# A hybrid decoder trunk: running sums carried in the accumulators, and the spatial gate's loads one block ahead

## The chip, the cores and the metric

The kernel runs on one core of a Trainium2 chip. The metric is device time in microseconds (us), and the figure for a kernel is the median of its timed executions. One further execution was taken under the hardware profiler. Its trace says when each instruction of each engine ran, and every row shown below comes from it.

The engines: TensorE (PE) multiplies matrices into PSUM, a memory of accumulators. VectorE (DVE) and ScalarE (ACT) work elementwise on SBUF and PSUM. SyncE (SP) issues the DMA transfers. Each engine works through its own queue in order.

## The reference

Two decoder layers run over 256 tokens of width 2048, in float32. The change lies in layer 0: in its input projection with the spatial gating that follows, and in its feed-forward network (FFN).

```
def swiglu(h, w_gate, w_up, w_down):
    a = silu(h @ w_gate) * (h @ w_up)
    return a @ w_down

def chunked_spatial_gating(u, v, ln_g, ln_b, w_s, b_s):
    v = layer_norm(v, ln_g, ln_b).reshape(bsz, n_chunks, 128, 16, 128)
    w = where(causal, w_s, 0.0)
    mixed = einsum('hts,bcshe->bcthe', w, v) + b_s.T[:, :, None]
    return u * mixed

def ab_mixer(hm, ...):
    u, v, z, xbc, dt_raw = split(hm @ w_in)
    y_a = chunked_spatial_gating(gelu(u), gelu(v), ...)
    y_b = ssd_mixer(z, xbc, dt_raw, ...)     # conv and silu of xbc, scan, silu(z)
    return concatenate([y_a, y_b]) @ w_out

# per layer
hm = rms_norm(x) * (1 + sc_m) + sh_m         # sc, sh, g: silu(c) @ ada_w + ada_b
x = x + (1 + g_m) * mixer(hm)
hf = rms_norm(x) * (1 + sc_f) + sh_f
x = x + (1 + g_f) * swiglu(hf)
```

## The kernel before

Every large product runs on TensorE in three passes. Weights and activations are split into a high and a low part: ScalarE rounds a slab of weights to its high part (`hi`, line 330), VectorE subtracts to get the low part (`lo`, line 335), and TensorE sums high by high, high by low and low by high in PSUM. A slab has up to two k tiles of 128 rows and 512 columns. `wslab` (line 320) loads it from SP into one of four `raw` buffers; `hi` and `lo` have three buffers each. A block is 512 output columns for all 256 tokens and fills one accumulator of 128 x 1024 in the pool `psA`, which has two. `dense_ws` keeps weights stationary and `dense_as` activations; their products are lines 396 and 162.

The modulation of a layer (`ada_w`) is itself streamed and summed on VectorE in the background (`ada_unit`, line 207). The first layer's input projection cannot wait for all of it. So `grouped` (line 548) cuts the 16 k tiles into groups of 4, 5 and 7 (`GROUPS`) and runs all 14 blocks of `ORDER` (six x, four v, four z) over the first group, then over the second, then over the third. The activations of a group are made at its start (`begin`, `adaln`, line 529). The running sum of a block rests in SBUF: after the first group ScalarE copies the accumulator out (line 584), after each later group VectorE adds the accumulator to it (line 586). Only behind the last group's add does `finish(i)` run. For a layer-0 input block that is `finish0`: the convolution and Silu of an x block (lines 861 to 869), Gelu of a v block with sums for the layer norm (line 987), Silu of a z block (line 990). The first six gate and six up blocks of the FFN of layer 0 go through the same function in two groups of 8 k tiles, with `finishf` (Silu, and product of the pair, lines 1308 and 1311). That is 14 copies and 28 adds in the first stage, 12 and 12 in the second.

The spatial gate is worked in behind chosen blocks. After block 9 of the third group (`LN_AT`) `layer_norm` reduces the sums, squares the four v tiles on ScalarE and takes a square root (lines 933 to 943). After blocks 9, 11, 12 and 13 (`GM_AT`) `layer_norm_apply(b)` loads gain and bias and applies them on VectorE (lines 952, 953), and `spatial(b)` loads four heads of 128 x 128 spatial weights (line 957), transposes them on TensorE (line 960), masks them on VectorE (line 962) and multiplies. These three loads are issued where they are used, into the pool `t2` with six buffers.

A planner places the instructions of each engine at build time, by their order in the program and by priorities (`tc.high_priority`), and that order is fixed in each queue. `tc.issue_after` puts an instruction behind another one on its engine.

Of the kernel before, what the change touches and what calls it, by code (L numbers as in the profile page):

```python
# [46 lines left out]
DEFER = 6  # L47
ORDER = ("x4", "v0", "x5", "v1", "x0", "v2", "x1", "v3", "x2", "z0", "x3", "z1", "z2", "z3")
LN_AT = 9
GM_AT = (9, 11, 12, 13)  # L50
SSD_AT = (12, 14, 18, 20)


# [1 line left out]
def trunk(ctx: ExitStack, tc: tile.TileContext, x, c, norm_mix_g, norm_ffn_g, ada_w, ada_b,  # L55
# [134 lines left out]
    def ada_unit(layer, base, stride, width, dst, nr=2):  # L190

        side = 2 if nr == 1 else 1
        wide = side * width
        nk = max(1, 1024 // wide)
        row = ada_w.shape[2]
        acc = adp.tile([P, 1024], F32, tag="acc", name="acc", bufs=2)[:, 0:wide]

        def use(raw, g0):  # L200
            for i in range(nk):
                g = g0 + i
                r = raw[:, i * wide:(i + 1) * wide]
                if g == 0:
                    V.tensor_scalar(acc, r, ct[nr][:, g:g + 1], None, op0=OP.mult)
                else:
                    V.scalar_tensor_tensor(acc, r, ct[nr][:, g:g + 1], acc, op0=OP.mult, op1=OP.add)  # L207

        def end():
            n = width // P  # L210
            if nr == 1:
                first_mod.append(acc)
                return
            total = tmp.tile([P, 32], F32, tag="tot", name="tot", bufs=2)[:, 0:nr * n]
            for j0 in range(0, n, 4):
                m = min(4, n - j0)
                ps = pm()
                for j in range(m):
                    transpose(ps[:, j * P:(j + 1) * P], acc[:, (j0 + j) * P:(j0 + j + 1) * P])
                V.tensor_reduce(total[:, nr * j0:nr * (j0 + m)].rearrange("p (j b) -> p j b", b=nr),  # L220
                                ps[:, 0:m * P].rearrange("p (j r b) -> p j b r", j=m, b=nr), axis=AX.X, op=OP.add)
            for b, (sec, k0) in enumerate(dst):
                r = total[:, b:nr * n:nr]
                V.scalar_tensor_tensor(mod[layer][sec][:, k0:k0 + n], r, 0.0 if sec in (0, 3) else 1.0,
                                       adab[layer][:, sec * KT + k0:sec * KT + k0 + n], op0=OP.add, op1=OP.add)
                have.update((layer, sec, k) for k in range(k0, k0 + n))
            if dst[0][0] in (2, 5):
                gate_to_rows(layer, dst[0][0])

        for g0 in range(0, KT * nr, nk):  # L230
            raw = (bt() if nr == 1 and g0 not in FIRST_A else
                   adp.tile([P, 1024], F32, tag="araw", name="araw", bufs=A_BUFS))
            for i in range(nk):
                r = raw[:, i * wide:(i + 1) * wide]
                if nr == 1:
                    r = r.rearrange("p (b n) -> p b n", b=2)
                off = ada_w.offset + (layer * D + (g0 + i) * (P // nr)) * row + base
                t = nc.sync.dma_start(r, bass.AP(tensor=ada_w.tensor, offset=off,
                                                 ap=[[row, P // nr], [stride, max(nr, 2)], [1, width]]))
                if nr == 1:  # L240
                    wlast[0] = t
            landed.append((slab[0], lambda raw=raw, g0=g0: use(raw, g0)))
            yield raw
        landed.append((slab[0], end))
# [130 lines left out]
        for j in js:  # L375
            preps.append(lambda j=j: turn(j, src[j // 2], make))

    def dense_ws(w, c0, ks, ahead=W_AHEAD):

        acc = psA.tile([P, 1024], F32, tag="acc", name="accps").rearrange("p (n t) -> p n t", n=4)  # L380
        done = 0
        for run in slabs(ks):
            run_prep()
            hi, lo = wslab(w, run[0][0], len(run), c0, 512, ahead)
            ops = []
            for i, (_, (bh, bl)) in enumerate(run):
                done += 1
                ops += [(hi[:, i, :], bh, done == 1, False), (hi[:, i, :], bl, False, False),
                        (lo[:, i, :], bh, False, done == len(ks))]
            if done <= 2:  # L390
                order = [(n, o) for i in (0, 2, 1) for n in range(4) for o in ops[i:i + 1]] \
                    + [(n, o) for n in range(4) for o in ops[3:]]
            else:
                order = [(n, o) for i in range(0, len(ops), 3) for n in range(4) for o in ops[i:i + 3]]
            for n, (a, b, first, final) in order:
                dense_mm[0] = T.matmul(acc[:, n, :], a[:, n * P:(n + 1) * P], b, start=first and n % 2 == 0,  # L396
                                       stop=final, skip_group_check=True)
            if done >= min(DEFER, len(ks)):
                run_later()
            pump()  # L400
        return acc
# [12 lines left out]
            with tc.issue_after(dense_mm[0].ins):  # L414
                dense_mm[0] = held.pop(0)()

    def dense_as(w, c0, ks, ahead=W_AHEAD, head=None, tail=False, hold=False):

        if tail:
            accs = [pm(), pm()]
        else:
            full = psA.tile([P, 1024], F32, tag="acc", name="accps").rearrange("p (n t) -> p n t", n=2)
            accs = [full[:, 0, :], full[:, 1, :]]
        runs = list(slabs(ks))
        parts = [runs[:2]] if head else []
# [3 lines left out]
        for pi, part in enumerate(parts):  # L431
# [15 lines left out]
            for n, j, (r, i, x) in order:  # L447
# [6 lines left out]

                def product(n=n, j=j, i=i, x=x, bh=bh, bl=bl, hi=hi, lo=lo, last=pi == len(parts) - 1):
                    return mm(accs[n], (bl if x == 1 else bh)[:, n * P:(n + 1) * P], (lo if x == 2 else hi)[:, i, :],
                              first=pi == 0 and j == 0, last=last and j == len(ops) - 1)

                if hold and len(part) > 1 and n == 1 and j >= len(ops) - 2:
                    held.append(product)  # L460
# [84 lines left out]
    xs = []  # L545
    fdst = []

    def grouped(blocks, groups, layer, sh, make, finish, rates, lags, heads=None, early=0):


        hs = []
# [1 line left out]
        def begin(gi):  # L553
# [5 lines left out]
                new_pace(QUIET if sh else 0)  # L559
            hs.extend(make(k0, kg))  # L560

        for gi, (k0, kg) in enumerate(groups):
            if not (early and gi):
                begin(gi)
# [3 lines left out]
            for i, (dense, w, c0, dst) in enumerate(blocks):  # L568
                if early and not last and i == len(blocks) - early:
                    begin(gi + 1)  # L570
                args = {"head": heads} if heads and gi == 0 and i == 0 else {}
                if not ks:
                    acc = opening(w, c0, kg)
                    hs.extend(hm)
# [3 lines left out]
                if dst is None:  # L578
                    if gi == 0:
                        fdst.append(tb())  # L580
                    dst = fdst[i]
                with tc.high_priority(offset=600):
                    if gi == 0:
                        A.activation(dst, acc, AF.Copy)
                    else:
                        V.tensor_tensor(dst, acc, dst, op=OP.add)  # L586
# [56 lines left out]
    def opening(w, c0, n):  # L643
# [65 lines left out]
                yield  # L709
                run("V", lambda: V.scalar_tensor_tensor(h[k][1], xs[k], g[k], t, op0=OP.mult, op1=OP.subtract))  # L710

        acc = psA.tile([P, 1024], F32, tag="acc", name="accps").rearrange("p (n t) -> p n t", n=4)

        def products(k):
            for i, (a, b) in enumerate(((hi[k], h[k][0]), (lo[k], h[k][0]), (hi[k], h[k][1]))):
# [217 lines left out]
    def layer_norm():  # L933
# [8 lines left out]
        A.activation(rv, rv, AF.Sqrt, bias=eps5, scale=1.0 / D)  # L942
        V.reciprocal(rv, rv)

    def layer_norm_apply(b):
        gB = t2()
        nc.sync.dma_start(gB, gm_ln_g[:, 512 * b:512 * (b + 1)].partition_broadcast(P))
        bB = t2()
        nc.sync.dma_start(bB, gm_ln_b[:, 512 * b:512 * (b + 1)].partition_broadcast(P))
        for cc in range(2):  # L950
            v = vt[b][:, cc, :]
            V.scalar_tensor_tensor(v, v, nmu[:, cc:cc + 1], gB, op0=OP.add, op1=OP.mult)
            V.scalar_tensor_tensor(v, v, rv[:, cc:cc + 1], bB, op0=OP.mult, op1=OP.add)

    def spatial(b):
        wraw = t2().rearrange("p (h s) -> p h s", h=4)
        nc.sync.dma_start(wraw, gm_w_s[0, 4 * b:4 * b + 4].rearrange("h t s -> t h s"))
        ps = pm()
        for h in range(4):
            T.transpose(ps[:, h * P:(h + 1) * P], wraw[:, h, :], ident)  # L960
        w = t2().rearrange("p (h t) -> p h t", h=4)
        V.tensor_tensor(w, ps.rearrange("p (h t) -> p h t", h=4), triu[:, None, :].to_broadcast([P, 4, P]),
                        op=OP.mult)
# [11 lines left out]
        for j in range(4):  # L975
            ssqy.add(zb[g][:, j, :])

    def finish0(i):
        kind, j = (ORDER[i][0], int(ORDER[i][1])) if i < len(ORDER) else ("", 0)
        if kind == "x":  # L980
            with tc.high_priority(offset=600):
# [1 line left out]
                    conv(4 * j + t)  # L983
        elif kind == "v":
            t = vt[j]
            for cc in range(2):
                A.activation(t[:, cc, :], t[:, cc, :], AF.Gelu_apprx_tanh, accum_out=sums[:, cc, j:j + 1])
        elif kind == "z":
            with tc.high_priority(offset=600):
                A.activation(zb[j], zb[j], AF.Silu)  # L990
        if i == LN_AT:
            layer_norm()
        for b in range(4):
            if GM_AT[b] == i:
                layer_norm_apply(b)
                spatial(b)
# [8 lines left out]
        queue_sec(l, sec, n)  # L1005
    rate[1] = 2.0
    smalls.append(small_loads())
    grouped(blocks0, GROUPS, 0, 0, make0, finish0, RATES, LAGS)
    ksm = [(k, hm[k]) for k in range(KT)]
    rate[0] = RATE  # L1010
    ya = {}
# [289 lines left out]
        fblocks.append((dense_as, ffn_w_gate[0], 512 * b, None))  # L1301
        fblocks.append((dense_as, ffn_w_up[0], 512 * b, None))

    def finishf(i):
        t = fdst[i]
        with tc.high_priority(offset=600):
            if i % 2 == 0:
                A.activation(t, t, AF.Silu)
            else:
                sg = fdst[i - 1]  # L1310
                V.tensor_tensor(sg, t, sg, op=OP.mult)
                ffn_split(sg, 4 * (i // 2), a)

    hf = grouped(fblocks, FGROUPS, 0, 3, makef, finishf, F_RATES, (LAGS[-1], LAGS[-1]), normf.head, 2)
    ffn_in(0, hf, 4 * FPAIRS, 6 - FPAIRS, a)
    ffn_out(0, a)
    a = []
# [195 lines left out]
```

## Time and profile before

| | us |
|---|---|
| median of 3 runs | 2564.55 (2564.42 to 2566.23) |
| profiled execution | 2565.73 |
| its span, first to last instruction | 2563.9 |
| TensorE busy | 2528.8 (99%) |
| VectorE busy | 1862.2 (73%) |
| ScalarE busy | 1265.6 (49%) |

The span runs from the first to the last instruction of the profiled execution. A busy share is an average over stages, so each stage has to be looked at by itself. Matmuls overlap in their pipeline; a busy TensorE need not run at its peak, and the granted clock says at which share of full speed it was allowed to run.

### The profile page before, as it was taken

To read this page: it belongs to the slowest core of one execution; us is meant where nothing else is said; L and a number is where in the kernel's file an instruction comes from. 1 tells how busy PE (TensorE), PEld (TensorE's weight loads), DVE (VectorE), ACT (ScalarE), POOL (GpSimd) and SP (SyncE) were. 2 spreads that over 40 slices of the span, in tenths; PEclk is the share of its full clock that TensorE was granted. 3 is DMA by queue.
4 is the path that set the end of the run, shared out by engine and by line. 5 is a ranking of instruction groups with operands and counts; after the bars stand their busy time and mean duration, and the time that the engine had idled before them with its cause. 6 is when DMAs were issued, how large, how long until landed. Compare 5 with 4: busy or idle time off the path is not lost.

```text
span 2563.9 us, 33519 instructions
## 1 busy us (share of the span) xinstructions
PE 2528.8 (99%) x12485; PEld 2128.0 (83%) x12485; DVE 1862.2 (73%) x1993; ACT 1265.6 (49%) x1640; POOL 6.5 (0%) x19
## 2 busy tenths in 40 slices
PE   7999989999999999999999999999999999999999
PEld 6999888878788888888888788888788888888887
DVE  6799888899878888777777777677764455545454
ACT  5534766555545444344444665554744443344443
POOL 0000000000000000000000000000000000000000
PEclk9999999999999999999999999999999999999999
DMA  8999668998799989999988688878676656666664
GB/s 325 321 343 328 185 202 259 309 318 297 264 326 329 314 302 310 325 316 302 302 308 304 223 282 261 272 263 282 197 257 196 192 189 200 204 190 189 188 204 166
DMA packets 309630, 676.01 MB, mean 264 GB/s; under 512 B 24272, under 2 KB 26842, under 8 KB 309466
## 3 DMA queue, kind: packets, MB, share of 16 engines
q1 hardware_dynamic: 309338, 673.85, 79.2%
q8 instruction: 98, 1.61, 0.2%
q14 instruction: 66, 0.54, 0.1%
q10 hardware_dynamic: 128, 0.02, 0.0%
HBM read 671.62 MB, written 2.16 MB: 263 GB/s over the span
## 4 chain that ended last, share of the span: by engine, by line
PE 96%; DVE 1%; DMA 1%; ACT 1%; issue 0%; SPq 0%; DVEq 0%; ACTq 0%
PE accps L162 79%; PE accps L396 8%; PE pm L162 6%; PE pm L153 2%; DMA t<-in_gm_w_s 1%; DVE acc L207 0%; DMA blk<-in_ada_w 0%; ACT hi L330 0%; DVE lo L335 0%; DMA raw<-in_ffn_w_gate 0%; DVE t L867 0%; PE pm L887 0%; ACT t L939 0%; DVE t L1145 0%; ACT h L1141 0%
## 5 line engine op out<-in xcount | busy, mean ns | idle before, releaser
L330 ACT ACTIVATE hi<-raw 128x1024 fp32r<-128x1024 f32 (+1 forms) x864 | 903.6, 1047 | 1177.1 <-PE accps L162 1016.8
L335 DVE TENSOR_TENSOR lo<-raw,hi 128x1024 fp32r<-128x1024 f32 (+1 forms) x864 | 1040.3, 1206 | 578.1 <-ACT hi L330 571.4
L162 PE MATMUL accps<-hi,h 128*128 128x512 f32 x2224 | 603.8, 392 | 0.0
L162 PE MATMUL accps<-lo,h 128*128 128x512 f32 x2224 | 600.4, 391 | 0.0
L162 PE MATMUL accps<-hi,l 128*128 128x512 f32 x2224 | 599.9, 390 | 0.0
L162 PEld LDWEIGHTS accps<-hi,l 128*128 128x128 f32 x2224 | 416.5, 188 | 87.1 <-issue 0.8
L162 PEld LDWEIGHTS accps<-lo,h 128*128 128x128 f32 x2224 | 415.4, 188 | 87.1 <-issue 1.6
L162 PEld LDWEIGHTS accps<-hi,h 128*128 128x128 f32 x2224 | 412.6, 188 | 83.3 <-issue 0.6
L207 DVE SCALAR_TENSOR_TENSOR acc<-araw,ct,acc 128x1024 f32<-128x1024 f32 (+2 forms) x377 | 465.3, 1234 | 2.7 <-DMA araw<-in_ada_w 2.0
L162 PE MATMUL accps<-hi,blk 128*128 128x512 f32 x1440 | 357.4, 390 | 0.0
L162 PEld LDWEIGHTS accps<-hi,blk 128*128 128x128 f32 x1440 | 269.5, 188 | 55.5
L162 PE MATMUL accps<-lo,blk 128*128 128x512 f32 x720 | 192.6, 389 | 0.0
L396 PE MATMUL accps<-h,lo 128*128 128x256 f32 x624 | 164.0, 287 | 3.1 <-DVE lo L335 3.1
L396 PE MATMUL accps<-h,hi 128*128 128x256 f32 x624 | 163.7, 286 | 2.3 <-ACT h L529 1.7
L396 PE MATMUL accps<-l,hi 128*128 128x256 f32 x624 | 163.2, 286 | 0.4 <-DVE l L530 0.4
L162 PEld LDWEIGHTS accps<-lo,blk 128*128 128x128 f32 x720 | 135.1, 188 | 28.0
L396 PEld LDWEIGHTS accps<-h,hi 128*128 128x128 f32 x624 | 115.2, 193 | 4.5 <-ACT h L529 1.9
L396 PEld LDWEIGHTS accps<-h,lo 128*128 128x128 f32 x624 | 114.7, 194 | 4.7 <-DVE lo L335 3.5
L396 PEld LDWEIGHTS accps<-l,hi 128*128 128x128 f32 x624 | 115.0, 195 | 0.8 <-DVE l L530 0.6
L162 PE MATMUL pm<-hi,blk 128*128 128x512 f32 x224 | 57.0, 390 | 0.6 <-ACT hi L330 0.6
L586 DVE TENSOR_TENSOR blk<-accps,blk 128x1024 f32<-128x1024 f32 x40 | 48.7, 1218 | 3.8 <-PE accps L162 2.6
L162 PEld LDWEIGHTS pm<-hi,blk 128*128 128x128 f32 x224 | 42.0, 188 | 9.8 <-ACT hi L330 1.1
(277 smaller groups left out, 1319.4 us busy)
## 6 DMA issues: line engine op xcount, KB each, us to landing
araw<-in_ada_w SPq DMA_DIRECT2D x323, 512.0 KB, 5.6
raw<-in_ffn_w_gate SPq DMA_DIRECT2D x176, 512.0 KB, 4.5
raw<-in_ffn_w_up SPq DMA_DIRECT2D x176, 512.0 KB, 4.5
raw<-in_ffn_w_down SPq DMA_DIRECT2D x176, 512.0 KB, 4.4
raw<-in_ab_w_in SPq DMA_DIRECT2D x128, 512.0 KB, 5.0
raw<-in_cd_w_in SPq DMA_DIRECT2D x96, 512.0 KB, 4.7
raw<-in_ab_w_out SPq DMA_DIRECT2D x64, 512.0 KB, 5.5
raw<-in_cd_w_out SPq DMA_DIRECT2D x32, 512.0 KB, 5.0
```

The costliest lines, as they stand in the source:

```text
L153: return T.transpose(dst, src, ident)
L162: return T.matmul(o, a, b, start=first, stop=last, skip_group_check=True)
L207: V.scalar_tensor_tensor(acc, r, ct[nr][:, g:g + 1], acc, op0=OP.mult, op1=OP.add)
L330: A.activation(hi, raw, AF.Copy)
L335: wlast[1] = V.tensor_tensor(lo, raw, hi.bitcast(F32), op=OP.subtract)
L396: dense_mm[0] = T.matmul(acc[:, n, :], a[:, n * P:(n + 1) * P], b, start=first and n % 2 == 0, stop=final, skip_group_check=True)
L586: V.tensor_tensor(dst, acc, dst, op=OP.add)
```

## The change

Behind the first group, a block no longer adds its running sum on VectorE. ScalarE copies the running sum from SBUF into the block's accumulator before the block starts (a seed), and no product of the block starts the accumulator anew. `reserve` takes the accumulators of a block and of the next one and writes the seeds, so a seed stands in the program one block ahead. After a middle group ScalarE copies the accumulator out again. After the last group `finish` reads the accumulator directly: Gelu for v, Silu for z, Silu and the product for the FFN. The x blocks' last group isn't seeded and keeps its add. Gelu gets the raised priority that the others had.

The loads of the spatial gate move into `load_gm(b)`, called behind the block before the one where they are used. Gain and bias go to the pool of the residual's gate (two buffers), the spatial weights in two halves to a buffer of their own and to the slot that held the last input tile. The blocks behind which the gate is worked become 9, 11, 13 and 15. The modulation's `total` moves from a pool of its own to `t1`.

```
-GM_AT = (9, 11, 12, 13)
+GM_AT = (9, 11, 13, 15)
...
-            total = tmp.tile([P, 32], F32, tag="tot", name="tot", bufs=2)[:, 0:nr * n]
+            total = t1()[:, 0:nr * n]
...
+    def acc_tile():
+        return psA.tile([P, 1024], F32, tag="acc", name="accps")
+
+    def dense_ws(w, c0, ks, ahead=W_AHEAD, into=None, seeded=False):
+        acc = (into or acc_tile()).rearrange("p (n t) -> p n t", n=4)
...
-                dense_mm[0] = T.matmul(acc[:, n, :], a[:, n * P:(n + 1) * P], b, start=first and n % 2 == 0,
+                dense_mm[0] = T.matmul(acc[:, n, :], a[:, n * P:(n + 1) * P], b, start=first and n % 2 == 0 and not seeded,
...
-                              first=pi == 0 and j == 0, last=last and j == len(ops) - 1)
+                              first=pi == 0 and j == 0 and not seeded, last=last and j == len(ops) - 1)
...
+        order = [(gi, i) for gi in range(len(groups)) for i in range(len(blocks))]
+        accs = {}
+
+        def seeded(gi, i):
+            return gi > 0 and (gi < len(groups) - 1 or direct(i))
+
+        def reserve(at):
+            n = order.index(at)
+            for gi, i in order[n:n + 2]:
+                if (gi, i) not in accs:
+                    accs[gi, i] = acc_tile()
+                    if seeded(gi, i):
+                        dst = blocks[i][3] if blocks[i][3] is not None else fdst[i]
+                        with tc.high_priority(offset=600):
+                            A.activation(accs[gi, i], dst.rearrange("p n t -> p (n t)"), AF.Copy)
+            return {"into": accs[at], "seeded": seeded(*at)}
...
+                if last and direct(i):
+                    finish(i, acc)
+                    continue
                 with tc.high_priority(offset=600):
-                    if gi == 0:
+                    if not last:
                         A.activation(dst, acc, AF.Copy)
                     else:
                         V.tensor_tensor(dst, acc, dst, op=OP.add)
...
+    def load_gm(b):
+        t = gm_loads[b] = [tmp.tile([P, 512], F32, tag="gate", name="gm", bufs=2) for _ in range(2)]
+        t += [tmp.tile([P, S], F32, tag="wg", name="wg", bufs=1), hp.tile([P, S], F32, tag="l%d" % KT, name="wg")]
+        with tc.issue_after(wlast[0].ins):
+            nc.sync.dma_start(t[0], gm_ln_g[:, 512 * b:512 * (b + 1)].partition_broadcast(P))
+            nc.sync.dma_start(t[1], gm_ln_b[:, 512 * b:512 * (b + 1)].partition_broadcast(P))
+            for i in range(2):
+                nc.sync.dma_start(t[2 + i].rearrange("p (h s) -> p h s", h=2),
+                                  gm_w_s[0, 4 * b + 2 * i:4 * b + 2 * i + 2].rearrange("h t s -> t h s"))
...
-            for cc in range(2):
-                A.activation(t[:, cc, :], t[:, cc, :], AF.Gelu_apprx_tanh, accum_out=sums[:, cc, j:j + 1])
+            with tc.high_priority(offset=600):
+                for cc in range(2):
+                    A.activation(t[:, cc, :], acc[:, cc, :], AF.Gelu_apprx_tanh, accum_out=sums[:, cc, j:j + 1])
         elif kind == "z":
             with tc.high_priority(offset=600):
-                A.activation(zb[j], zb[j], AF.Silu)
+                A.activation(zb[j], acc, AF.Silu)
...
         for b in range(4):
+            if GM_AT[b] == i + 1:
+                load_gm(b)
             if GM_AT[b] == i:
                 layer_norm_apply(b)
                 spatial(b)
...
-    grouped(blocks0, GROUPS, 0, 0, make0, finish0, RATES, LAGS)
+    grouped(blocks0, GROUPS, 0, 0, make0, finish0, RATES, LAGS, lambda i: ORDER[i][0] != "x")
...
-    def finishf(i):
-        t = fdst[i]
+    def finishf(i, acc):
         with tc.high_priority(offset=600):
             if i % 2 == 0:
-                A.activation(t, t, AF.Silu)
+                A.activation(fdst[i], acc, AF.Silu)
             else:
                 sg = fdst[i - 1]
-                V.tensor_tensor(sg, t, sg, op=OP.mult)
+                V.tensor_tensor(sg, acc, sg, op=OP.mult)
                 ffn_split(sg, 4 * (i // 2), a)
```

## Rows read from the trace of the kernel before

**Rows 1.** The page: engines' busy time, and the chain of waits by engine.
```profile
PE 2528.8 (99%) x12485; PEld 2128.0 (83%) x12485; DVE 1862.2 (73%) x1993; ACT 1265.6 (49%) x1640; POOL 6.5 (0%) x19
...
PE 96%; DVE 1%; DMA 1%; ACT 1%; issue 0%; SPq 0%; DVEq 0%; ACTq 0%
```

**Rows 2.** TensorE's waits, 38 to 400 us: total, times, longest.
```profile
PE pm L960 <- DMA t<-in_gm_w_s: 3.6, 2, 2.3
PE accps L396 <- DVE lo L335: 3.1, 2, 2.4
PE accps L396 <- ACT h L529: 1.7, 1, 1.7
PE accps L396 <- ACT hi L330: 0.6, 1, 0.6
```

**Rows 3.** Stretches: length, busy us by engine, TensorE's granted clock, DMA share, GB/s.
```profile
119.00:130.00 11.00, 8.89 (x59) 8.47 (x58) 10.88 (x22) 6.37 (x10) 0.00 (x0) 0.84 0.75 247
...
300.00:325.00 25.00, 25.00 (x171) 23.17 (x171) 21.37 (x34) 21.26 (x40) 0.00 (x0) 1.00 0.70 197
325.00:336.00 11.00, 6.38 (x52) 5.97 (x51) 8.02 (x17) 9.73 (x19) 0.00 (x0) 1.00 0.68 202
336.00:346.00 10.00, 9.19 (x62) 8.99 (x63) 9.71 (x15) 5.77 (x9) 0.00 (x0) 0.83 0.62 181
...
830.00:965.00 135.00, 135.00 (x622) 112.23 (x621) 117.23 (x109) 63.54 (x66) 0.00 (x0) 1.00 0.91 310
```

**Rows 4.** Timeline of TensorE, 326 to 339 us: start, duration, idle time before.
```profile
329.70 0.66 PE L960 MATMUL pm<-ident,t 128*128 128x128 f32 x4 [2.33 <-DMA t<-in_gm_w_s]
...
336.07 0.39 PE L396 MATMUL accps<-h,lo 128*128 128x256 f32 x1 [2.37 <-DVE lo L335]
...
338.26 1.06 PE L396 MATMUL accps<-h,lo 128*128 128x256 f32 x4 [0.74 <-DVE lo L335]
```

**Rows 5.** Timeline of VectorE, 304 to 336 us.
```profile
304.49 1.22 DVE L586 TENSOR_TENSOR blk<-accps,blk 128x1024 f32<-128x1024 f32 x1
...
322.85 1.22 DVE L586 TENSOR_TENSOR blk<-accps,blk 128x1024 f32<-128x1024 f32 x1
...
330.45 0.69 DVE L962 TENSOR_TENSOR t<-pm,triu 128x512 f32<-128x512 f32 x1 [2.98 <-PE pm L960]
...
334.67 0.75 DVE L952 SCALAR_TENSOR_TENSOR blk<-blk,nmu,t 128x512 f32<-128x512 f32 x1
335.33 0.68 DVE L335 TENSOR_TENSOR lo<-raw,hi 128x512 fp32r<-128x512 f32 x1
```

**Rows 6.** The spatial weights' loads: SP's first issue, and landing of all four.
```profile
325.23 0.38 SPq L957 DMA_DIRECT2D t<-in_gm_w_s  x1
...
DMA to landing us min/median/max: 4.4/5.9/7.3
```

**Rows 7.** Lines 584, 586 and 1308: durations in ns, min/median/max.
```profile
L584 ACT ACTIVATE blk<-accps x26: 1001/1008/1030, 45.5 to 826.1; 128x1024 f32<-128x1024 f32 x26
...
L586 DVE TENSOR_TENSOR blk<-accps,blk x40: 1211/1218/1225, 133.7 to 962.1; 128x1024 f32<-128x1024 f32 x40
...
L1308 ACT ACTIVATE blk<-blk x6: 1061/1062/1063, 838.4 to 952.5; 128x1024 f32<-128x1024 f32 x6
```

**Rows 8.** Timeline of ScalarE, 119 to 343 us.
```profile
119.99 1.02 ACT L584 ACTIVATE blk<-accps 128x1024 f32<-128x1024 f32 x1 [4.44 <-PE accps L396]
121.04 1.09 ACT L529 ACTIVATE h<-xs,mod,gs 128x256 fp32r<-128x256 f32 x2
...
314.68 0.40 ACT L869 ACTIVATE blk<-t 128x256 f32<-128x256 f32 x1
315.10 1.28 ACT L987 ACT_TABLE_LOAD   x1
316.40 0.63 ACT L987 ACTIVATE blk<-blk 128x512 f32<-128x512 f32 x1
...
342.92 1.04 ACT L990 ACTIVATE blk<-blk 128x1024 f32<-128x1024 f32 x1
```

More of the change, by code (lines that the diff above doesn't have):

```diff
@@ L376, in queue_turns @@
             preps.append(lambda j=j: turn(j, src[j // 2], make))
-    def dense_ws(w, c0, ks, ahead=W_AHEAD):
-        acc = psA.tile([P, 1024], F32, tag="acc", name="accps").rearrange("p (n t) -> p n t", n=4)
+    def acc_tile():
+        return psA.tile([P, 1024], F32, tag="acc", name="accps")
+    def dense_ws(w, c0, ks, ahead=W_AHEAD, into=None, seeded=False):
+        acc = (into or acc_tile()).rearrange("p (n t) -> p n t", n=4)
         done = 0
@@ L415, in run_held, with dense_as @@
                 dense_mm[0] = held.pop(0)()
-    def dense_as(w, c0, ks, ahead=W_AHEAD, head=None, tail=False, hold=False):
+    def dense_as(w, c0, ks, ahead=W_AHEAD, head=None, tail=False, hold=False, into=None, seeded=False):
         if tail:
@@ L423, in dense_as @@
         else:
-            full = psA.tile([P, 1024], F32, tag="acc", name="accps").rearrange("p (n t) -> p n t", n=2)
+            full = (into or acc_tile()).rearrange("p (n t) -> p n t", n=2)
             accs = [full[:, 0, :], full[:, 1, :]]
@@ L546, in trunk, with grouped @@
     fdst = []
-    def grouped(blocks, groups, layer, sh, make, finish, rates, lags, heads=None, early=0):
+    def grouped(blocks, groups, layer, sh, make, finish, rates, lags, direct, heads=None, early=0):
         hs = []
@@ L570, in grouped @@
                     begin(gi + 1)
-                args = {"head": heads} if heads and gi == 0 and i == 0 else {}
+                args = reserve((gi, i)) if ks else {}
+                if heads and gi == 0 and i == 0:
+                    args["head"] = heads
                 if not ks:
@@ L710, in rest @@
                 run("V", lambda: V.scalar_tensor_tensor(h[k][1], xs[k], g[k], t, op0=OP.mult, op1=OP.subtract))
-        acc = psA.tile([P, 1024], F32, tag="acc", name="accps").rearrange("p (n t) -> p n t", n=4)
+        acc = acc_tile().rearrange("p (n t) -> p n t", n=4)
         def products(k):
@@ L943, in layer_norm @@
         V.reciprocal(rv, rv)
+    gm_loads = {}
+    def load_gm(b):
[7 more added lines that the diff above has]
+                                  gm_w_s[0, 4 * b + 2 * i:4 * b + 2 * i + 2].rearrange("h t s -> t h s"))
     def layer_norm_apply(b):
[L946 to L949, printed above, removed]
+        gB, bB = gm_loads[b][0:2]
         for cc in range(2):
@@ L955, in spatial @@
     def spatial(b):
-        wraw = t2().rearrange("p (h s) -> p h s", h=4)
-        nc.sync.dma_start(wraw, gm_w_s[0, 4 * b:4 * b + 4].rearrange("h t s -> t h s"))
+        wraw = gm_loads[b][2:4]
         ps = pm()
         for h in range(4):
-            T.transpose(ps[:, h * P:(h + 1) * P], wraw[:, h, :], ident)
+            T.transpose(ps[:, h * P:(h + 1) * P], wraw[h // 2][:, (h % 2) * P:(h % 2 + 1) * P], ident)
         w = t2().rearrange("p (h t) -> p h t", h=4)
@@ L976, in ssd_out, with finish0 @@
             ssqy.add(zb[g][:, j, :])
-    def finish0(i):
+    def finish0(i, acc=None):
         kind, j = (ORDER[i][0], int(ORDER[i][1])) if i < len(ORDER) else ("", 0)
@@ L1302, in trunk @@
         fblocks.append((dense_as, ffn_w_up[0], 512 * b, None))
-    def finishf(i):
-        t = fdst[i]
+    def finishf(i, acc):
         with tc.high_priority(offset=600):
             if i % 2 == 0:
-                A.activation(t, t, AF.Silu)
+                A.activation(fdst[i], acc, AF.Silu)
             else:
                 sg = fdst[i - 1]
-                V.tensor_tensor(sg, t, sg, op=OP.mult)
+                V.tensor_tensor(sg, acc, sg, op=OP.mult)
                 ffn_split(sg, 4 * (i // 2), a)
-    hf = grouped(fblocks, FGROUPS, 0, 3, makef, finishf, F_RATES, (LAGS[-1], LAGS[-1]), normf.head, 2)
+    hf = grouped(fblocks, FGROUPS, 0, 3, makef, finishf, F_RATES, (LAGS[-1], LAGS[-1]), lambda i: True,
+                 normf.head, 2)
     ffn_in(0, hf, 4 * FPAIRS, 6 - FPAIRS, a)
```

## The prediction, made before the change was run

> **What bounds the kernel now.** I read the page's engine table and its chain first: TensorE is busy for 2528.8 us of the span and 96% of the chain is TensorE [rows 1]. So an edit counts only where TensorE stands still, or runs at a lower clock, in the two stages that the change touches. I then asked for TensorE's waits in the first of them, from the first dense product to the end of the three groups (38 to 400 us) [rows 2]. The whole of it is 9.4 us (9.0 in the four rows shown): 3.6 us for the loads of the spatial weights (2.3 for the first, 1.3 left for another), 3.1 us for low parts (line 335), 1.7 us for the second group's first operand (line 529), 0.6 us for a high part. No row names an accumulator: no block has to wait until its accumulator is evacuated. In the last group of the FFN stage TensorE is busy 135.00 of 135.00 us [rows 3], so nothing can be won there.
>
> The table by stretches shows where the 6.7 us lie and what follows them. From 325 to 336 us TensorE is busy only 6.38 of 11.00 us, and from 336 to 346 us its granted clock is 0.83, which is 1.7 us of ten [rows 3]; the same is seen after the wait at the second group's start (0.84 in 119 to 130 us) [rows 3]. VectorE and ScalarE are full ahead of the stall: 21.4 and 21.3 of 25 us [rows 3]. The timelines then tell the order. TensorE reaches the transposes of the first spatial weights at 327.4 us and starts them at 329.70 [rows 4]; their load was issued at 325.23 [rows 6]. VectorE's triangular mask (line 962) stands at the head of its queue all that time, idle 2.98 us, and the convolutions, the next block's layer norm (line 952) and the low part at 335.33 come behind it [rows 5]. That low part is what TensorE waits for next, 2.37 us and then 0.74 [rows 4]. So one late load is paid three times: by TensorE itself, through VectorE's queue, and by the clock.
>
> **The change part by part.**
>
> *Adds become seeds.* Of 40 adds (line 586) VectorE loses 34: 14 in the second group, 8 (the v and z blocks) in the third, 12 in the FFN stage; at 1.218 us [rows 7] that is 41.4 us. ScalarE gains 34 seeds and the 14 evacuations of the second group. No row shows ScalarE writing PSUM. The nearest are the evacuation of the same shape out of PSUM, 1.008 us, and Silu from SBUF to SBUF, 1.06 us [rows 7]; I take 1.06, the dearer end, so 48 x 1.06 = 51 us. None of the 41.4 us was waited for by TensorE except through the low parts, and none of the 51 us need be: a block of the third group lasts about 9.2 us (the adds at 304.49 and 322.85 are two blocks apart [rows 5]), and a seed needs only the time of one evacuation and one write, 2.1 us, within it. The cover is the block in between, as there are two accumulators; without it each seed would cost TensorE about 2 us, 34 x 2 = 68 us. The time of a product that adds instead of writes has no row of its own, but most products of every block already add; I take nothing, either way.
>
> *At a group's start* the seed of its second block becomes ready as the last evacuation ends (119.99 + 1.02 us), just when ScalarE is to make the first operand, at 121.04 [rows 8]. TensorE waits for that operand. If the seed goes first it costs up to 1.06 us, at two group starts 0 to 2.1 us; I take 0.5, since the third group's start showed no wait.
>
> *Gelu and Silu read the accumulator.* The instructions are the same; they drop one step (the add) but now hold the accumulator. Before, Gelu and Silu ran when ScalarE had time: the last v block was added at 304.49 and its Gelu ran at 316.40; the first z block was added at 322.85 and its Silu ran at 342.92 [rows 5, 8]. Run at each block's end, Gelu alternates with the convolutions' Silu, so I count up to three more table loads of 1.28 us, 3.9 us of ScalarE between 225 and 345 us. ScalarE's lag reached TensorE for 0.6 us [rows 2]; that wait may vanish (-0.6) or become that of two loads (+2.6). I take +0.6. A load takes 1.28 us and the instructions beside it follow at once: one begins at 314.68 and lasts 0.40, the load runs at 315.10, Gelu at 316.40 [rows 8]. The Trainium skill ("ScalarE: Activation LUTs", section "What ACT_TABLE_LOAD costs") counts a drain of some 1.38 us with each load, 2.66 us in all; by it three more switches would be 8.0 us of ScalarE instead of 3.9, an estimate from the page, and the term would lean to its upper end. This trace shows no such drain: 0.02 us on either side.
>
> *The gate's loads a block ahead.* Four transfers for three on SP, 0.4 us of issue each, and the load of block b+1 is issued after the weights of the block before. Landing took 4.4 to 7.3 us [rows 6], a block lasts 9.2, so the load should be there: the wait of 3.6 us goes, all of it. The low parts' 3.1 us go with their cause only in part: TensorE comes to them 2.3 us earlier too, and VectorE is then 2.98 us earlier. What tips it is that VectorE also loses the add at 322.85 (1.22 us) and the next block's layer norm at 334.67 (0.75 us twice), which moves behind the later load [rows 5]. I take 2.3 of 3.1, and 1.3 of the clock's 1.7 us; both ends are nothing and all. What the new place of the loads can cost: they use the two gate buffers and one weight buffer each, so SP stands at the load of block b+1 until VectorE and TensorE have used block b's, and the weight loads queue behind. Four raw buffers cover that, some 10.5 us of products (an estimate: a block of 9.2 us is three and a half slabs). The sums' tile moves from a pool of its own to the t1 pool: VectorE may wait for a free one; no TensorE wait hangs on it after 130 us, so nothing.
>
> *Sum:* -3.6 - 2.3 - 1.3 + 0.5 + 0.6 = -6.1 us. The profiled execution took 2565.73 us (span 2563.9 and 1.8 around it), so 2559.6; it lies 1.2 us over the median of 2564.55, so against the median 2558.5.
>
> **Rivals.**
>
> *The stall only moves.* The load is early, but layer norm (eight Squares, a Sqrt with its table load, two VectorE passes) is not, and TensorE waits for its result or for a low part behind it. For: ScalarE and VectorE were full from 300 to 336 us [rows 3] and ScalarE gets two seeds and a Silu more there. Against: Gelu of the last v block, on which layer norm hangs, comes about 10 us earlier. Only the 3.6 us are won, 0.5 + 0.6 lost and some 1 us of the clock: about -1.5 us, 2563.
>
> *Slower: the accumulator is held.* If Gelu or Silu stay as late as they were, the accumulator is not free, the seed two blocks on is late and TensorE waits. The last v block's Gelu, two halves of 0.63 from 316.40, ended at 317.7; with the seed 318.8, while the block two on began at about 313.6 (9.2 us before the add at 322.85): 5.2 us. The first z block's Silu ended at 343.98, with the seed 345.0, against a start two blocks on at about 339.2 (322.85, a block of 9.2 us, waits of 2.3 + 2.4 + 0.7 and 1.7 of the clock): 5.8 us. With a clock dip of 1.7 us behind each and the 3.6 us of the loads won, 5.2 + 5.8 + 3.4 - 3.6 = +10.8 us, 2575.4. It decides from the point where ScalarE gets to the evacuation more than 9.2 - 2.1 = 7.1 us after the block's last product. For it: that is what the trace of before shows twice, and Silu was raised in its priority even then. Against: Gelu is newly raised, the seed behind it too, and a planner that sees TensorE wait puts them first.
>
> *The change does nothing.* The load is issued no earlier than before because its buffers come free late: then -0 to -1 us, 2564.
>
> **How the numbers follow.** Forecast 0.55; the stall moves or nothing changes 0.27 together; slower 0.18. A measurement of this kernel can tell about 0.2%, 5.1 us, from no change. The forecast's own span, from its terms' ends, is -9 us (3.6 + 3.1 + 1.7 + 0.6 all won) to -1 us (3.6 won, 2.1 and some lost); about 0.44 of its 0.55 lies beyond 5.1 us. The slower case reaches past +5.1 us in most of its 0.18. So faster 0.45, same 0.40, slower 0.15. The range goes to 2554.0 below (-10.5, a little of the second group's wait and its clock dip won as well) and to 2570.0 above, half way into the slower case.
>
> **What would show it.** Right: no wait of line 960 for the spatial weights in TensorE's waits; low-part waits under 1 us in the third group; a granted clock of 1.00 from 330 to 346 us; 34 adds gone from VectorE and 34 seeds of about 1.0 us on ScalarE with no TensorE wait for a seed. Wrong: a TensorE wait for the seed or for a Gelu or Silu; a wait of SP for gate buffers longer than the weights' cover; a longer wait for line 529's operand; or the old wait under a new name near 330 us, in layer norm.

## The result: 20 us slower, and the profile after

The changed kernel takes 2584.5 us (median; 2582.61 to 2586.78) against 2564.42 us for the kernel before on the same chip: ratio 1.0077, 95% interval 1.0063 to 1.0092. The forecast was 2558.5 with a range up to 2570.0. The profiled execution took 2583.69 us, 18.0 us over the one of before; its span is 2581.0 us, 17.1 over.

The page of the changed kernel: engines' busy time, to be held against [rows 1].

```profile
span 2581.0 us, 33534 instructions
...
PE 2532.6 (98%) x12485; PEld 2130.4 (83%) x12485; DVE 1828.3 (71%) x1959; ACT 1312.6 (51%) x1691; POOL 6.3 (0%) x19
```

The work itself changed as planned: VectorE has 34 instructions fewer and ScalarE is busy 47 us longer. TensorE's busy time hardly moved. What moved is its waiting. TensorE's waits of the changed kernel, 38 to 410 us, answer to [rows 2]; the last row comes from 800 to 860 us, in the FFN stage:

```profile
PE accps L400 <- ACT blk L1024: 13.6, 4, 4.9
PE accps L400 <- DVE lo L335: 3.3, 2, 1.9
PE pm L996 <- DMA wg<-in_gm_w_s: 2.6, 2, 2.0
PE accps L400 <- ACT blk L612: 1.9, 1, 1.9
PE accps L400 <- ACT blk L1027: 0.6, 1, 0.6
...
PE accps L162 <- ACT blk L612: 0.7, 1, 0.7
```

Line 400 is the product of an x or z block (396 before), 1024 is Gelu, 1027 Silu, 612 the copy out of an accumulator. Before, no row named an accumulator; now 16.8 us are spent waiting for one to be evacuated, at seven block starts. Gelu alone holds TensorE four times, for 13.6 us. The totals of the old waits hardly moved, 2.6 us instead of 3.6 for the spatial weights and 3.3 instead of 3.1 for low parts, but the low parts' waits lie elsewhere. Before, they were at 336 and 338 us [rows 4]. Now they end at 124.1 and 219.5 us, at the second group's start and at its end, and none is left in the third group:

```profile
124.09 0.39 PE L400 MATMUL accps<-h,lo 128*128 128x256 f32 x1 [1.36 <-DVE lo L335]
...
219.53 0.39 PE L400 MATMUL accps<-h,lo 128*128 128x256 f32 x1 [1.92 <-DVE lo L335]
```

From 210 to 219.5 us ScalarE is busy for 9.47 of 9.50 us. The 1.7 us for the second group's operand are gone; TensorE comes there later, behind the wait of 1.9 us for the copy.

At each long wait of the third group, in it or right behind it, the clock falls for a stretch. The third group of the changed kernel by stretches (columns as in [rows 3]; the last but two is the granted clock):

```profile
250.00:262.00 12.00, 7.93 (x49) 7.69 (x49) 4.68 (x14) 4.46 (x8) 0.00 (x0) 0.72 0.50 148
262.00:280.00 18.00, 15.38 (x92) 13.34 (x91) 16.46 (x32) 17.50 (x26) 0.00 (x0) 0.98 0.49 148
280.00:290.00 10.00, 9.18 (x57) 9.18 (x58) 2.94 (x4) 4.87 (x11) 0.00 (x0) 0.69 0.59 179
290.00:306.00 16.00, 13.05 (x72) 11.04 (x70) 13.45 (x20) 11.85 (x18) 0.00 (x0) 1.00 0.52 152
306.00:316.00 10.00, 9.68 (x68) 9.68 (x69) 1.86 (x2) 3.96 (x7) 0.00 (x0) 0.83 0.37 126
...
330.00:342.00 12.00, 11.04 (x81) 11.04 (x82) 4.58 (x9) 11.94 (x28) 0.00 (x0) 0.86 0.36 111
...
354.00:368.00 14.00, 11.43 (x80) 10.83 (x80) 8.56 (x12) 6.29 (x10) 0.00 (x0) 0.88 0.53 152
```

Length times what the clock lacks gives 3.4 + 0.4 + 3.1 + 1.7 + 1.7 + 1.7 = 12.0 us, against 3.5 before (1.8 in 119 to 130 us and 1.7 in 336 to 346). The ledger: waits 22.0 + 0.7 against 9.4 is 13.3 us, the clock 8.5, together 21.8 us; the spans differ by 17.1. Two corrections close most of the gap. First, 1.9 us of the clock's loss fell while TensorE was waiting anyhow (the granted clock was 0.80, 0.79 and 0.90 within the waits that end at 254.07, 280.82 and 330.96 us), so they are counted twice. Second, the profiled execution of before ran at a clock of 0.57 from 34 to 42 us, 3.4 us lost, where this one had 1.00; 1.5 us of that show as an earlier first dense product (36.3 against 37.8 us from the span's start). That leaves 16.5 us of the 17.1. The other eight profiled executions had this early dip too, at 0.57 to 0.79, so it is not put down to the change.

**Which block waits, and why.** The first of the four, on three engines, 242 to 256 us of the changed kernel. VectorE adds the first x block (x4) out of its accumulator; ScalarE writes a seed, converts weights, and runs Gelu of the first v block (v0); TensorE starts the next x block (x5):

```profile
242.86 1.22 DVE L614 TENSOR_TENSOR blk<-accps,blk 128x1024 f32<-128x1024 f32 x1
...
244.11 1.03 ACT L582 ACTIVATE accps<-blk 128x1024 f32<-128x1024 f32 x1 [2.01 <-DVE blk L614]
...
250.38 1.06 ACT L330 ACTIVATE hi<-raw 128x1024 fp32r<-128x1024 f32 x1 [2.42 <-DMA raw<-in_ab_w_in]
251.46 1.28 ACT L1024 ACT_TABLE_LOAD   x1
252.75 0.60 ACT L1024 ACTIVATE blk<-accps 128x512 f32<-128x512 f32 x1
...
253.34 0.59 ACT L1024 ACTIVATE blk<-accps 128x512 f32<-128x512 f32 x1
...
254.07 1.22 PE L400 MATMUL accps<-h,hi 128*128 128x256 f32 x4 [4.92 <-ACT blk L1024]
```

The seed at 244.11 waited for the add of x4 and for nothing else: it was written into the accumulator that x4 had just left. But that seed belongs to v1, the block after x5. The only other accumulator holds v0. So x5, which stands next in TensorE's queue and needs no seed, must wait until Gelu has read v0. By the turns that I had assumed, x5 should have had the one that x4 left, at 244.1, and v1 the other.

So the pool gives out whichever accumulator is free to whichever instruction is placed first; the program's order of requests, in which x5 stood ahead of v1, didn't decide it. Before, the only writers of accumulators were blocks of products in TensorE's one queue, so requests came in the blocks' order. A seed is a writer on another engine, raised in priority and ready as soon as its source is. Wherever an unseeded block is followed by a seeded one, the seed can overtake. There are eight such places and seven waits: x5, x0, x1 and x2 behind a v block (Gelu), x3 behind a z block (Silu), and the last block of the first group in each of the two stages (copy). The eighth is x4, the third group's first block, behind z3 of the second group. The seed of v0 ran ahead of it too:

```profile
218.59 1.01 ACT L582 ACTIVATE accps<-blk 128x1024 f32<-128x1024 f32 x1
```

But TensorE had other products to do (lines 157 to 159) from 223.7 us until x4 began at 228.92, and z3's accumulator was copied out by 225.8 us, so nothing waited.

### The profile page after: what moved, and what is told of

Read it like the earlier page. It is cut to its first block, busy times and chain, and to the rows that moved or that the text cites. A ratio compares the mean times of both kernels' runs of the same rounds, so it can differ in the third digit from the quotient of the medians.

```text
span 2581.0 us, 33534 instructions
## 1 busy us (share of the span) xinstructions
PE 2532.6 (98%) x12485; PEld 2130.4 (83%) x12485; DVE 1828.3 (71%) x1959; ACT 1312.6 (51%) x1691; POOL 6.3 (0%) x19
## 4 chain that ended last, share of the span: by engine, by line
PE 87%; ACT 1%; DVE 1%; DMA 0%; issue 0%; ACTq 0%
PE accps L162 76%; PE pm L162 6%; PE accps L400 3%; PE pm L153 2%; DMA raw<-in_ffn_w_gate 0%; PE pm L915 0%; ACT hi L330 0%; DVE t L1184 0%; ACT h L1180 0%; DVE xr L1087 0%; ACT t L1171 0%; DVE l L1188 0%; DVE blk L1084 0%; ACT blk L1024 0%; PE pm L1451 0%
## 5 line engine op out<-in xcount | busy, mean ns | idle before, releaser
L400 PE MATMUL accps<-h,hi 128*128 128x256 f32 x624 | 167.3, 292 | 16.1 <-ACT blk L1024 13.6
L612 ACT ACTIVATE blk<-accps 128x1024 f32<-128x1024 f32 x40 | 40.5, 1013 | 6.6 <-PE accps L162 3.3
```

## The experiments

Theory A is that: the accumulator is taken by the wrong block. Theory B is that ScalarE is simply too full with 48 more passes and Gelu's table loads. Theory C is that the loads of the spatial gate cost the time.

### Accumulators strictly in turn

```
+    turns = [0]
+
     def acc_tile():
-        return psA.tile([P, 1024], F32, tag="acc", name="accps")
+        turns[0] += 1
+        return psA.tile([P, 1024], F32, tag="acc%d" % (turns[0] % 2), name="accps", bufs=1)
```

> The changed kernel with one thing fixed: the two accumulators are taken strictly in turn (two tags of one buffer each), so a seed can't take the one that the block before it needs. Theory A (a seed takes the free accumulator ahead of an unseeded block, which then waits for the evacuation of its immediate predecessor): TensorE's waits for Gelu, Silu and copies (13.6, 0.6, 1.9 and 0.7 us) go to under 2 us together, the clock's dips behind them too, 2558 to 2566 us. Theory B (ScalarE is simply too full with Gelu, its table loads and 34 seeds): the same instructions run, so the waits stay, 2578 to 2587 us.

Measured: 2562.54 us against 2563.97, ratio 0.9992 (0.9982 to 1.0001). The whole loss is gone with ScalarE doing the same work. TensorE's waits of this kernel, 30 to 420 us:

```profile
PE accps L403 <- ACT h L536: 2.7, 1, 2.7
...
PE accps L403 <- ACT hi L330: 2.0, 2, 1.8
PE pm L157 <- ACT t L832: 1.4, 1, 1.4
PE accps L403 <- DVE lo L335: 0.7, 2, 0.5
...
PE pm L999 <- DMA wg<-in_gm_w_s: 0.2, 1, 0.2
```

No row for Gelu, Silu or a copy is left. On ScalarE's timeline of this kernel Gelu of v0 is as late as ever, but v1's seed now follows it, and x5 had the other accumulator:

```profile
252.80 1.28 ACT L1027 ACT_TABLE_LOAD   x1
254.09 0.60 ACT L1027 ACTIVATE blk<-accps 128x512 f32<-128x512 f32 x1
...
255.39 1.03 ACT L585 ACTIVATE accps<-blk 128x1024 f32<-128x1024 f32 x1
```

So it is not Gelu's lateness, nor ScalarE's load, but who waits for it. Theory A stands; B falls as the cause of the loss.

### The seeds alone

The gate's loads, `GM_AT` and the sums' tile as before; the rest of the change kept.

```
-GM_AT = (9, 11, 13, 15)
+GM_AT = (9, 11, 12, 13)
...
-            total = t1()[:, 0:nr * n]
+            total = tmp.tile([P, 32], F32, tag="tot", name="tot", bufs=2)[:, 0:nr * n]
...
-        gB, bB = gm_loads[b][0:2]
+        gB = t2()
+        nc.sync.dma_start(gB, gm_ln_g[:, 512 * b:512 * (b + 1)].partition_broadcast(P))
...
-            if GM_AT[b] == i + 1:
-                load_gm(b)
```

> The seeds and the direct reading of accumulators alone; the spatial gate's loads, their blocks and the sums' tile are as before. Theories A and B: the whole loss is in the seeds, 2578 to 2588 us, with four waits for Gelu of about 13 us in all. Theory C (the gate's loads and later blocks cost the time, through SP or layer norm): 2560 to 2567 us.

Measured: 2589.09 us, ratio 1.0099 (1.0084 to 1.0114). The loss is in the seeds, all of it and 5 us more, a little above the range that was expected. TensorE's waits of this kernel, 30 to 420 us:

```profile
PE accps L400 <- ACT blk L1016: 14.2, 4, 4.2
PE accps L400 <- DVE lo L335: 3.6, 2, 1.9
PE accps L400 <- ACT blk L1019: 3.4, 1, 3.4
...
PE accps L400 <- ACT blk L612: 1.9, 1, 1.9
```

The same four waits for Gelu (line 1016 here), and that for the first z block's Silu (1019) is 3.4 us instead of 0.6. Theory C falls.

### The gate's loads alone

The kernel before, with `load_gm`, the blocks 9, 11, 13 and 15, and `total` in `t1`.

```
-GM_AT = (9, 11, 12, 13)
+GM_AT = (9, 11, 13, 15)
...
+            if GM_AT[b] == i + 1:
+                load_gm(b)
             if GM_AT[b] == i:
                 layer_norm_apply(b)
```

> The kernel before with the other part alone: the gate's loads one block ahead, worked at blocks 9, 11, 13 and 15, the sums' tile in t1. Theories A and B: no wait for an evacuation, 2556 to 2566 us; as the prediction's steps had it 2559, with TensorE's wait for the spatial weights gone; if the transposes only move up with their load, a wait of 2 to 3 us for it stays and the time is 2562 to 2566. Theory C: over 2575 us.

Measured: 2565.76 us, ratio 1.0005 (0.9996 to 1.0014): no difference that can be told. TensorE's waits of this kernel, 30 to 420 us, and then ScalarE's timeline ahead of the one of 3.6 us:

```profile
PE accps L396 <- ACT hi L330: 5.3, 4, 3.6
...
PE accps L396 <- ACT h L529: 1.7, 1, 1.7
PE accps L396 <- DVE lo L335: 0.8, 1, 0.8
```

```profile
365.40 1.28 ACT L910 ACT_TABLE_LOAD   x1
...
368.39 1.28 ACT L998 ACT_TABLE_LOAD   x1
...
371.93 1.28 ACT L915 ACT_TABLE_LOAD   x1
373.22 0.42 ACT L915 ACTIVATE t<-bc 128x256 f32<-128x256 f32 x1
373.54 1.04 ACT L330 ACTIVATE hi<-raw 128x1024 fp32r<-128x1024 f32 x1
```

The part does what it says: TensorE's wait for the spatial weights is gone (3.6 us before), and that for low parts fell from 3.1 to 0.8. But TensorE waits 5.3 us for high parts instead of 0.6, most of it in one wait of 3.6 us that ends at 374.63, some 45 us behind the stall that was removed. The scan's exponentials (lines 910 and 915 here) and a block's Silu (line 998) lie ahead of the weights' conversion at 373.54, each with its table load. Before, the first load for line 910 came at 381.01; presumably the gate's later work left room in which the planner put it earlier, but no run isolates that. One kind of wait was traded for another, and the clock dips at that one too: 0.94 from 346 to 400 us is 3.2 us, where the old stall cost 1.7.

### The seeds alone, accumulators in turn

The two edits above together: the gate as before, and the tags in turn.

> The seeds alone, with the accumulators strictly in turn. Theory A: as fast as before or a little faster, 2558 to 2566 us, no wait for Gelu over 1 us. Theory B: 2576 to 2588 us. Its difference to the first run of this call is what the gate's loads are worth once nothing else is in the way.

Measured: 2561.87 us, ratio 0.9993 (0.9984 to 1.0003). There is no wait for Gelu, and 1.2 us are left for the spatial weights, now once. Beside the first experiment (0.9992) the gate's loads are worth nothing that can be measured.

### Every block of the third group seeded

```
         def seeded(gi, i):
-            return gi > 0 and (gi < len(groups) - 1 or direct(i))
+            return gi > 0
...
-                    if not last:
-                        A.activation(dst, acc, AF.Copy)
-                    else:
-                        V.tensor_tensor(dst, acc, dst, op=OP.add)
+                    A.activation(dst, acc, AF.Copy)
```

> The changed kernel with the x blocks of the third group seeded too (six more seeds, and six copies out by ScalarE in place of six adds by VectorE). ScalarE has some 12 us more to do; the accumulators are not fixed. Theory A (an unseeded block loses the free accumulator to the seed behind it): in the third group every block now claims its accumulator by its own seed in order, so the waits of 13.6 and 0.6 us go, while the two at the ends of the first groups stay (1.9 and 0.7): 2562 to 2571 us. Theory B (ScalarE is too full): worse than the changed kernel, 2588 us and more.

Measured: 2570.79 us against 2563.07, ratio 1.0027 (1.0016 to 1.0037). TensorE's waits of this kernel, 38 to 420 us, and two of its stretches:

```profile
PE accps L400 <- ACT hi L330: 7.6, 4, 3.0
PE accps L400 <- DVE lo L335: 2.1, 4, 1.0
PE accps L400 <- ACT blk L611: 1.9, 1, 1.9
```

```profile
300.00:325.00 25.00, 23.20 (x151) 20.80 (x151) 13.19 (x20) 23.55 (x33) 0.00 (x0) 1.00 0.69 215
325.00:336.00 11.00, 7.40 (x55) 6.79 (x55) 4.51 (x8) 10.97 (x25) 0.00 (x0) 0.97 0.13 35
```

ScalarE is busy 15.7 us longer than in the changed kernel (1328.3 against 1312.6), and the kernel loses 0.27% where that one loses 0.77%: the waits for Gelu and Silu are gone, since no unseeded block of the third group is left to be overtaken. The wait at the first group's end (line 611, 1.9 us) stays, as theory A has it: an unseeded block with a seeded one behind it. Theory B has a small part in it: here ScalarE really is full (23.55 of 25 us, 10.97 of 11), and TensorE waits 7.6 us for high parts.

### Each block reserves only its own accumulator

```
-            for gi, i in order[n:n + 2]:
+            for gi, i in order[n:n + 1]:
```

> The changed kernel, but a block reserves and seeds only its own accumulator, not the next one's as well. Theory A: the seed is then behind the block before it in the program and all seven waits go, 2558 to 2566 us, like the run with accumulators in turn. If a raised priority were enough for a seed to overtake, waits for Gelu stay: 2575 us and more.

Measured: 2561.26 us, ratio 0.9995 (0.9986 to 1.0004). It is one character of the change, and it undoes the loss as well as the turns do. The rows for Gelu, Silu and copies are gone from TensorE's waits; of the seeds' own lateness one wait is left, 38 to 420 us:

```profile
PE accps L400 <- ACT h L533: 2.7, 1, 2.7
...
PE accps L400 <- ACT accps L582: 0.7, 1, 0.7
```

So the raised priority alone doesn't let a seed overtake; it takes the reserving one block ahead. Whether that would do without the raised priority, no run shows. And the block ahead isn't needed: a seed that comes only with its own block is late once, by 0.7 us.

### The second block's seed behind the group's operands

On top of the turns; first with the gate's loads, then with the gate as before.

```
-                        with tc.high_priority(offset=600):
+                        with tc.high_priority(offset=600), (tc.issue_after(pace[-1][0]) if gi and pace and i < 2 else ExitStack()):
```

> The changed kernel with the accumulators strictly in turn, and at a group's start the second block's seed queued behind the group's operands. In the first run with accumulators in turn, that seed ran just ahead of the second group's first operand, and TensorE waited 2.7 us for the operand against 1.7 before. If the seed was the cause, the wait falls back to about 1.7 and the time by 1 us, 2559 to 2563. If not, the wait stays at 2.7.

> The seeds alone (the gate as before), with accumulators in turn and the second block's seed behind the operands. It should be the fastest of all if the gate's loads bring nothing: 2558 to 2562 us, a little under the kernel before. If the gate's loads are worth something once TensorE is no longer held, it is 1 to 3 us slower than the other run with this queue order.

Measured: 2562.3 us, ratio 0.9998 (0.999 to 1.0007), and 2561.39 us, ratio 0.9996 (0.9988 to 1.0005). With plain turns the seed ran right ahead of the second group's first operand. ScalarE's timeline of the first experiment, and then TensorE's wait for that operand in the two kernels of this section:

```profile
119.52 1.02 ACT L615 ACTIVATE blk<-accps 128x1024 f32<-128x1024 f32 x1 [3.38 <-PE accps L403]
120.58 1.03 ACT L585 ACTIVATE accps<-blk 128x1024 f32<-128x1024 f32 x1
121.54 1.08 ACT L536 ACTIVATE h<-xs,mod,gs 128x256 fp32r<-128x256 f32 x2
```

```profile
PE accps L403 <- ACT h L536: 1.7, 1, 1.7
```

The wait fell from 2.7 to 1.7 us as expected, but not the time: waits for high and low parts came to 4.3 and 3.9 us where plain turns had 2.7 and 1.9. That the second kernel is the fastest of all, as was expected, can't be told: it lies 0.9 us under the first and 0.1 us over the one of the section before, both within the noise. So here too the gate's loads are worth nothing that can be measured. No version can be told to beat the kernel before. The intervals of six of the eight reach 1; the two others, the seeds alone (1.0099) and every block seeded (1.0027), are slower.

## Why the prediction was wrong, step by step

**What bounds the kernel.** Right: TensorE's waits and its clock decide, and the ledger of the loss, made of those two alone, comes to 16.5 us of the 17.1 between the spans.

**Adds become seeds: the step that failed.** The counts held (34 instructions off VectorE). A seed takes 1.028 us (median of 34) where I took 1.06 from the nearest row, and ScalarE's busy time rose by 47.0 us where I had 51 and 3.9 for tables. VectorE lost 33.9 us busy where I had 41.4. Most of both differences is in the counting: busy time counts a stretch in which two instructions overlap only once, and my sums added durations. Added up by duration, VectorE lost 42.0 us and ScalarE gained 52.0.

What failed is the sentence on the cover, "the block in between, as there are two accumulators". I took it that two accumulators are used by turns. Before, they were used so, but only since TensorE's queue was their only writer; nothing in the program holds them to it. The question to ask of that cover was what makes the turns; they go with the first writer on another engine. The runs show the step in both directions: with the turns fixed by tags the ratio is 0.9992, with the reservation only at the block itself 0.9995, against 1.0077.

Even the price that I gave for a lost cover, about 2 us a place, was near: the seven waits come to 2.4 us each, and the clock adds up to half as much again (8.5 to 16.8, with 1.9 of it inside the waits). That closeness is luck: I had priced one evacuation and one seed in line, and the seven waits, each for the evacuation of the block just before, run from 0.6 to 4.9 us. I had also put at nothing what TensorE waits for ScalarE's added time. The low parts' waits at 124.1 and 219.5 us lie in the second group, where ScalarE got 28 of its 48 passes; whether the passes caused them, no run isolates.

**Gelu and Silu read the accumulator.** The rival that I called "the accumulator is held" is the right kind, and I had it at 0.18. I let the late Gelu hold up the block two on, through its seed, at the last v block and the first z block: 10.8 us in all. In fact it is the very next block, at all four v blocks and the first z block. It need not even be late for that: from the end of v0's last product, at about 249 us, TensorE would have waited for Gelu however soon it ran. The point from which I said it decides, 7.1 us after the block's end, is therefore wrong by a whole block: it decides from zero. Three more table loads came, as counted (31 in the changed kernel's instruction list, 28 before), but not for the reason given: only one of them is Gelu's (4 instead of 3), two are the z blocks' Silu (3 instead of 1). TensorE's wait for high parts doesn't appear among the changed kernel's waits, so of the two ends that I gave the lower came true there, with the accumulators hiding it; with the turns it is 2.0 us against 0.6, a rise of 1.4 between my ends of -0.6 and +2.6.

The load of the table took 1.28 us in the changed kernel too, and Gelu followed at 252.75 behind the load at 251.46, 0.01 us after its end. The Trainium skill's drain ("ScalarE: Activation LUTs", section "What ACT_TABLE_LOAD costs") doesn't show here either.

**At a group's start.** The mechanism was right at the second group's start, and there the price was at its upper end: with the turns the seed stands ahead of the operand and the wait rises by 1.0 us (I had up to 1.06 a start, and took 0.5 for both starts together); queued behind, it falls back. At the third group's start no such wait shows. In the changed kernel itself the second group's wait for the operand does not appear, as TensorE came late.

**The gate's loads.** The forecast's gain of 7.2 us (3.6 + 2.3 + 1.3) hung on this step. Alone, the part removes what it should: 3.6 us of waiting for the weights and 2.3 of the low parts' 3.1. But the time stayed (1.0005), since 4.7 us came back as waits for high parts, and the clock's dip at them costs more than the old one. That is the rival "the stall only moves", though not through layer norm as I had it. The step that failed is the assumption that what is late next is known once the present stall is gone: where ScalarE is full (11.91 of 12 us from 360 to 372 us in that run), the next thing late is another conversion.

In the changed kernel the low parts' wait did leave the third group, as forecast, but 2.6 us for the spatial weights stayed, 0.6 at 328.28 us and 2.0 at 356.44. I had their load a block ahead, 9.2 us; it is issued at 323.16 and 352.01, 5.1 and 4.4 us ahead of the transposes, and took 4.9 to 6.5 us to land. SP stands before it at weight loads that wait for a raw buffer (24.3 us in eleven waits for VectorE's low parts, 290 to 325 us). With the turns the first of the two loads has 7.4 us, and 0.2 us of waiting is left. The clock of 1.00 that I expected from 330 to 346 us was 0.86 from 330 to 342.

**What is open.** Why the versions with turns gain no more than 0.02 to 0.08%, which their intervals don't tell from nothing, with VectorE relieved of 34 us: TensorE hardly waited for VectorE, so little was to be had, but I didn't trace the waits for high parts that came instead to one cause. The planner's order changes with every edit, and 1.9 to 4.3 us of waits for high and low parts turn up in each of the versions with turns, at places that differ.

## What to carry to other kernels

When a new instruction on another engine becomes the first writer of a buffer from a small pool, ask what kept the pool in turn before; with this planner a pool gives its buffers to whoever is placed first, and a write reserved one block ahead can take the buffer of the block that runs next. In a trace it shows as a wait for the evacuation of the immediately preceding block; to test it give each turn a tag of its own, or reserve only when the block itself begins. And a stall beside two full engines is not a sum to be collected: take it away alone, and look at what is late next, before counting it.

## What the runs showed of the hardware

A wait of TensorE can cost more than its length. In the stretches of 10 to 12 us that hold the waits of 3 to 5 us in the changed kernel, or follow them, the granted clock was 0.69 to 0.83, that is, the clock spent part of them at 1.2 instead of 2.4 GHz, 1.7 to 3.4 us each. Length alone does not tell: the 1.9 us wait for Gelu that ends at 330.96 us had a dip (0.86 from 330 to 342 us), and the 1.9 us wait for a copy that ends at 112.80 had none (1.00 in the rows of 98 to 119 and 119 to 130 us of the changed kernel, 0.84 in the latter before, behind a wait of 1.7 us):

```profile
98.00:119.00 21.00, 19.06 (x160) 18.85 (x159) 16.23 (x23) 10.41 (x14) 0.00 (x0) 1.00 0.94 329
119.00:130.00 11.00, 9.64 (x71) 8.98 (x71) 11.00 (x17) 7.58 (x11) 0.00 (x0) 1.00 0.77 253
```

A ScalarE copy of 128 x 1024 from SBUF into PSUM took 1.007 to 1.032 us, out of PSUM into SBUF 1.000 to 1.031 us; the direction makes next to no difference.
